# Hybrid decoder step: state space parameters made early, two accumulators for the third gate's branches, half of that gate in seven products

## The chip, the cores and the metric

The kernel runs on 1 core of one Trainium2 chip. The metric is the time of one execution in microseconds (us) of the device, as the median of several runs. A trace of one execution, which a hardware profiler took, shows every instruction of the five engines: TensorE (PE), VectorE (DVE), ScalarE (ACT), GpSimd (POOL) and SyncE (SP, which here only issues transfers).

## What is computed

One layer of a decoder for 1056 tokens (1024 of a prompt, 32 of eight samples), width 1024. The state of eight samples comes in and goes out. Cut to the parts that matter here:

```python
h = layer_norm(x) * (1 + sc1) + sh1             # sc1, sh1, ... = silu(c) @ w_ada + b_ada
proj = h @ w_in                                 # columns for four token mixers
# (A) state space layer: 16 groups of 16 channels, 64 complex states each
dt = exp(log_dt); ab = exp(dt * a_re) * (cos(dt * a_im) + 1j * sin(dt * a_im))
bb = (ab - 1) / a * b                           # parameters: no token in them
state[t] = ab * state[t-1] + bb @ u[t]
y_s = real(c @ state) + d * u
y_s = gelu(y_s);  y_a = y_s * sigmoid(y_s @ w_glu)
# (B) short gated convolution -> y_b   (C) gated delta rule -> y_c   (D) stick-breaking attention -> y_d
br = einsum('blnw,nwd->blnd', stack([y_a, y_b, y_c, y_d]), w_branch)
gates = sigmoid(h @ w_gate)                     # 4 x 1024 columns
x = layer_norm(ALPHA * x + (1 + g1) * (sum(gates * br) @ w_o))
h2 = layer_norm(x) * (1 + sc2) + sh2
x = layer_norm(ALPHA * x + (1 + g2) * (swiglu(h2 @ w_ffn_up) @ w_ffn_down))
```

## The kernel before

Features lie on the partitions, tokens in the columns, in NTB = 3 blocks of TB = 352. Each factor of a large product is held as an fp16 pair hi and lo; `mm3` issues three fp16 products for one (hi with hi, hi with lo, lo with hi). `split` makes the pair: ACT writes hi, and DVE or POOL writes lo as the difference (L108, L114, L116, L118). A 128-column weight tile takes the way wraw (fp32, loaded by SP) to whl (fp16 pair).

The tiles are issued by a scheduler at build time. It orders each engine's instructions by priorities and modelled times; `with self.sup` marks work that goes ahead of all else, `with self.lo` products that fill.

The order of the program is: `make_h`; attention (D), and inside it the short convolution (B), `ssm_u` (which stores the state space layer's input u) and the first half of the gate of B (n = 1); the delta rule (C) with the other half; then the gate of D (n = 3), the gate of C (n = 2, here called the third gate), the state space layer `ssm` (A), the sums for the seven products, the gate of A (n = 0), the output projection `mixer_out` and `ffn`.

A gate is made in one of two ways. In `gates`, an m (128 of the 1024 columns) is a direct product: for each block 24 matmuls of 352 columns into a tile of the pool gps, six matmuls of `branch` (y with w_branch) into another tile of gps, tanh on ACT (gth, L1490), the product with the branch on DVE (gth, L1494) and an addition into mix on POOL. In `gates7`, two m are made as a pair by a two-by-two scheme with seven products instead of eight (`seven`); each of the seven takes sums of weight blocks, which `pair_weights` makes (four sums on DVE, L1635 to L1643; seven lo parts on POOL, L1631; hi parts on ACT), and sums of blocks of h, which `sums7` makes on DVE once for all pairs (L1711 to L1720, with splits at L116 into the tile tf). There are six calls of `sums7`. Three of the seven products take h itself and need no sum of h. With G7 = 4 the third gate is direct for all eight m, and only the gate of A goes in pairs.

`ssm` makes its parameters first: many small operations of 8 columns (tiles sp_*), powers of the rotation cs and sn on POOL (seven rounds of a complex product, 42 operations, L1220), the tables car, cai and ab on DVE, four groups of four transposes of ab into bq, and 64 small products into k0, which goes to DRAM as kd and is read back shifted as eight tt, to which DVE adds D (L1358). Then come products of u with bq (tile sps), the scan (gg, hr and hi on DVE), the output products with tt, car and cai (sps again), gelu (gs, gx), the product with w_glu, and y_A, which is split with a stride, since the token order of the scan is another than that of the gates. The direct products of the third gate are issued ahead of `ssm` in the program, and the scheduler lays them between its products.

`ada_slab` makes 128 of the columns that scale, shift and gate: 16 small products into a tile of gps, then ACT (adat, L294) and DVE (mod, L295), both of which read PSUM. `gates` calls it once per m, `gates7` several times per pair.

The lines that the argument touches are these:

```python
    B.gates(3, B.yD, False, False, ada=A3)
    B.gates(2, B.yC, False, False, range(2 * G7), ada=A2)
    B.ssm(yp)
    ...
            B.sums7(B.h, Tf, b, g7.tile([P, 8 * HB], F32, name="r7", tag="r7"), slice(q, q + 2))
    ...
    B.gates7(2, B.yC, False, range(G7, KD // 2))
    B.gates7(0, B.yA, True, range(KD // 2))
```

## Time and profile before

| | |
|---|---|
| median of 3 runs | 1919.74 us (1913.41 to 1923.58) |
| profiled execution | 1927.88 us |
| its span, first to last instruction | 1925.8 us |
| mean granted clock of TensorE | 0.961 |
| busy: PE, DVE, ACT, POOL | 1734.6, 1297.0, 970.8, 953.9 us |
| moved by transfers | 130.60 MB, mean 68 GB/s |

All positions below are in us from the start of the span. The stages around the change lie so: attention with convolution and `ssm_u` up to about 340, delta rule and gate of D to 735, third gate and state space layer from 735 to 933, sums and gate of A to 1071, then output projection and ffn. A row of a stretch gives each engine's busy time with the number of its instructions in brackets; idle time of an engine that nothing waits for costs nothing.

### The profile page before, as it was taken

The numbers are of one execution on the slowest core, as the hardware profiler recorded it, in microseconds if no ns is written. First come the engines' busy times: TensorE is split into PE (matmuls) and PEld (weight loads), VectorE is DVE, ScalarE is ACT, GpSimd is POOL, SyncE is SP. The second block draws the span as 40 slices with busy tenths as digits, with TensorE's granted clock in tenths as the row PEclk, the third lists the DMA queues.
The fourth block names the chain that finished last, engine by engine and source line by source line (L and its number), as shares of the span: only waits on it lengthen the run. The fifth ranks groups of instructions, "written<-read, shape, count | busy, mean of one in ns | idle before, by whom it ended". The sixth has DMA issues, their size and how long they took to land.

```text
span 1925.8 us, 36541 instructions
## 1 busy us (share of the span) xinstructions
PE 1734.6 (90%) x14985; PEld 1198.5 (62%) x14985; DVE 1297.0 (67%) x2161; ACT 970.8 (50%) x1796; POOL 953.9 (50%) x952
## 2 busy tenths in 40 slices
PE   7899999999899998788689899988999998999896
PEld 3466666656566665556367555556666776767675
DVE  6763777668676765386986479677467657755748
ACT  3642454465554645235664665645445644554434
POOL 1826421222354444744541553278577667675733
PEclk9999999999999999889799999989999999999999
DMA  8222220122311112313232340001121112111112
GB/s 310 75 90 64 73 59 23 49 58 54 96 50 58 62 40 98 73 41 102 77 110 77 129 137 1 1 23 44 48 64 56 48 44 65 56 37 53 50 28 91
DMA packets 63615, 130.60 MB, mean 68 GB/s; under 512 B 16408, under 2 KB 35928, under 8 KB 63192
## 3 DMA queue, kind: packets, MB, share of 16 engines
q1 hardware_dynamic: 61912, 124.07, 20.8%
q0 software_dynamic: 1536, 4.20, 0.7%
q8 instruction: 117, 1.92, 0.4%
q14 instruction: 50, 0.41, 0.1%
HBM read 117.36 MB, written 10.88 MB: 67 GB/s over the span
## 4 chain that ended last, share of the span: by engine, by line
PE 35%; DVE 26%; POOL 12%; ACT 10%; DMA 9%; issue 7%; SPq 1%; another core or an unknown queue 0%; ACTq 0%; DVEq 0%; POOLq 0%
PE gps L87 25%; DMA wraw<-in_w_up 3%; POOL wf L1631 2%; DVE x L1903 2%; POOL whl L1631 2%; DVE ring L116 2%; PE nps L87 1%; DMA wraw<-in_w_down 1%; DVE af L1869 1%; ACT wraw L1622 1%; DVE dacc L758 1%; POOL wraw L1635 1%; PE dp L87 1%; POOL wraw L1638 1%; POOL wraw L1639 1%
## 5 line engine op out<-in xcount | busy, mean ns | idle before, releaser
L87 PEld LDWEIGHTS <-whl 128*128 128x128 f16 x6992 | 623.5, 100 | 386.1 <-issue 74.9
L87 PE MATMUL gps<-h,whl 128*128 128x352 f16 (+1 forms) x4344 | 692.9, 314 | 49.0 <-ACT ct L1683 14.8
L87 PEld LDWEIGHTS <-wf 128*128 128x128 f16 x2232 | 197.7, 99 | 71.6 <-issue 13.8
L1631 POOL TENSOR_TENSOR wf<-wraw,wf 128x512 f16<-128x512 f32 (+1 forms) x102 | 122.8, 1206 | 145.8 <-ACT wf L1630 142.9
L1631 POOL TENSOR_TENSOR whl<-wraw,whl 128x512 f16<-128x512 f32 (+1 forms) x136 | 169.2, 1250 | 47.0 <-ACT whl L1630 46.8
L114 POOL TENSOR_TENSOR whl<-wraw,whl 128x1024 f16<-128x1024 f32 (+1 forms) x66 | 149.1, 2260 | 81.2 <-ACT whl L108 79.2
L105 ACT ACTIVATE wraw<-wraw 128x1024 f32<-128x1024 f32 (+2 forms) x96 | 96.4, 1005 | 127.4 <-DMA wraw<-in_w_gate 40.1
L87 PE MATMUL gps<-tf,whl 128*128 128x352 f16 (+1 forms) x1152 | 141.1, 280 | 18.6 <-ACT ct L1683 6.9
L1622 ACT ACTIVATE wraw<-wraw 128x1024 f32<-128x1024 f32 (+1 forms) x68 | 66.5, 978 | 111.0 <-DMA wraw<-in_w_up 62.2
L1630 ACT ACTIVATE whl<-wraw 128x512 f16<-128x512 f32 (+1 forms) x136 | 79.9, 589 | 78.8 <-POOL wraw L1635 34.5
L87 PE MATMUL gps<-ring,whl 128*128 128x352 f16 (+1 forms) x864 | 103.8, 276 | 13.1 <-DVE x L1903 13.1
L87 PE MATMUL gps<-y,wbr 128*128 128x352 f16 x576 | 105.4, 319 | 8.1 <-DVE gth L1771 3.8
L1680 DVE TENSOR_TENSOR ct<-ct,gps 128x352 f32<-128x352 f32 (+1 forms) x84 | 35.4, 424 | 106.5 <-PE gps L87 90.5
L1523 POOL TENSOR_TENSOR mix<-mix,gth 128x352 f32<-128x352 f32 x48 | 54.0, 1125 | 98.0 <-DVE gth L1494 87.1
L87 PE MATMUL gps<-mix,wo 128*128 128x352 f16 x576 | 88.8, 315 | 5.7 <-DVE gth L1771 3.4
L116 DVE TENSOR_TENSOR ring<-af,ring 128x352 f16<-128x352 f32 (+2 forms) x134 | 82.0, 645 | 7.8 <-ACT ring L108 7.7
L108 ACT ACTIVATE whl<-wraw 128x1024 f16<-128x1024 f32 (+1 forms) x82 | 84.8, 1035 | 4.4 <-DMA wraw<-in_w_ada 3.5
L87 PE MATMUL gps<-h,wf 128*128 128x352 f16 (+1 forms) x624 | 79.4, 283 | 6.6 <-DVE gth L1494 5.5
L87 PEld LDWEIGHTS <-wbr 128*128 128x128 f16 x576 | 56.5, 99 | 39.2 <-issue 10.2
L87 PEld LDWEIGHTS <-wo 128*128 128x128 f16 x576 | 56.7, 99 | 38.6 <-issue 5.9
L108 ACT ACTIVATE ring<-af 128x352 f16<-128x352 f32 (+2 forms) x134 | 52.2, 427 | 46.4 <-DVE af L1869 30.4
L87 PE MATMUL gps<-tf,wf 128*128 128x352 f16 (+1 forms) x528 | 66.6, 283 | 3.8 <-ACT cu L1683 3.6
(625 smaller groups left out, 3381.4 us busy)
## 6 DMA issues: line engine op xcount, KB each, us to landing
wraw<-in_w_up SPq DMA_DIRECT2D x44, 512.0 KB, 3.5
wraw<-in_w_gate SPq DMA_DIRECT2D x32, 512.0 KB, 3.9
wraw<-in_w_ada SPq DMA_DIRECT2D x32, 512.0 KB, 3.5
wraw<-in_w_in SPq DMA_DIRECT2D x20, 512.0 KB, 4.0
wraw<-in_w_down SPq DMA_DIRECT2D x24, 384.0 KB, 3.1
x<-in_xT SPq DMA_DIRECT2D x12, 704.0 KB, 7.7
araw<-in_w_ada SPq DMA_DIRECT2D x16, 512.0 KB, 10.9
wraw<-in_w_branch SPq DMA_DIRECT2D x8, 512.0 KB, 3.5
```

The source lines that it names most:

```text
L87: self.nc.tensor.matmul(out, lhsT=lhsT, rhs=rhs, start=start, stop=stop, skip_group_check=resume)
L105: nc.scalar.activation(src, src, AF.Copy, scale=scale)
L108: nc.scalar.activation(hi, src, AF.Copy, scale=scale)
L114: nc.gpsimd.tensor_tensor(lo, src, hi, op=ALU.subtract)
L116: nc.vector.tensor_tensor(lo, src, hi, op=ALU.subtract)
L758: nc.vector.scalar_tensor_tensor(acc[:, :L], ext[:, k:k + L], wts[:, i, k:k + 1], acc[:, :L], op0=ALU.mult, op1=ALU.add)
L1523: nc.gpsimd.tensor_tensor(o, o, g, op=ALU.add)
L1622: nc.scalar.activation(raw, raw, AF.Copy, scale=SW)
L1630: nc.scalar.activation(hi, src, AF.Copy)
L1631: nc.gpsimd.tensor_tensor(lo, src, hi, op=ALU.subtract)
L1680: add = lambda o, p: nc.vector.tensor_tensor(o, o, p, op=ALU.add)
L1903: nc.vector.scalar_tensor_tensor(x[:, h, z], part(h, z), gate[:, m, 0:1], x[:, h, z], op0=ALU.mult, op1=ALU.add)
```

## The change

1. G7 goes from 4 to 2. The third gate's m 0 to 3 stay direct, ahead of `ssm`; m 4 to 7 become two pairs in `gates7`, behind the six `sums7`. `ada_slab` is called four times less in `gates` and that many times more in `gates7`.
2. `gpb`, a PSUM pool of two banks, holds the branch products from the third gate until `ssm` is issued; in exchange sps has three banks instead of five.
3. The parameters of `ssm` move to `ssm_prep`, called in the attention ahead of `ssm_u`. Their results go to DRAM (spt, kd, with D already added in kd) and are loaded again at the head of `ssm`, before its products.
4. `ada_slab` copies all 18 columns out of PSUM with one ACT operation of top priority, and DVE adds from SBUF.
5. The tail of y_A is written in token order into a tile yt by two DVE operations, and one contiguous split follows for each half.

```diff
-G7 = 4
+G7 = 2
...
-            t = self.cp.tile([P, 9], F32, name="adat", tag="adat", bufs=2)
-            nc.scalar.activation(t, ps[:, 9:18], AF.Identity, scale=c, bias=self.b_ada[:, m:m + 1])
-            nc.vector.scalar_tensor_tensor(self.mod[:, m], ps[:, 0:9], c, t, op0=ALU.mult, op1=ALU.add)
+            t = self.cp.tile([P, 18], F32, name="adat", tag="adat", bufs=2)
+            with self.sup:
+                nc.scalar.activation(t, ps[:, 0:18], AF.Copy, scale=c)
+            nc.vector.scalar_tensor_tensor(self.mod[:, m], t[:, 0:9], self.b_ada[:, m:m + 1], t[:, 9:18],
+                                           op0=ALU.add, op1=ALU.add)
...
+    def ssm_prep(self):
...
+        def put(name, src, o=0):
+            d = self.spd(name)
+            nc.sync.dma_start(d[:, o:o + src.shape[1]], src)
...
+                V.tensor_tensor(k0[q, :, 112:128], k0[q, :, 112:128], dg[q], op=ALU.add)
+                nc.sync.dma_start(kd.rearrange("h (a e) c -> e h a c", e=2)[e][:, ha], k0[q])
...
-            p_ = pp.tile([P, 512], F32, name="sps", tag="sps", bufs=5)
+            p_ = pp.tile([P, 512], F32, name="sps", tag="sps", bufs=3)
...
+        with self.sup:
+            nc.sync.dma_start(U, self.su)
+            nc.sync.dma_start(bq.rearrange("p a j c -> p (a j c)"), self.spd("bq"))
+            nc.sync.dma_start(cs.rearrange("p a c -> p (a c)"), self.spd("cs"))
+            nc.sync.dma_start(sn.rearrange("p a c -> p (a c)"), self.spd("sn"))
+            nc.sync.dma_start(m8, self.spd("m8"))
+            for j in range(8):
+                nc.sync.dma_start(tt[16 * j:16 * j + 16], self.kd[:, :, 112 - 16 * j:240 - 16 * j])
+            nc.sync.dma_start(car.rearrange("p a k o -> p (a k o)"), self.spd("car"))
+            nc.sync.dma_start(cai.rearrange("p a k o -> p (a k o)"), self.spd("cai"))
+            nc.sync.dma_start(p4.rearrange("p i a -> p (i a)"), self.spd("p4"))
...
-            V.scalar_tensor_tensor(th, th, 1.0, ys[i], op0=ALU.add, op1=ALU.mult)
-            tv = th.rearrange("p (j c) -> p j c", j=8)
-            pv = lambda j: yA[:, j, i, 0:NP].rearrange("p (c j) -> p j c", j=8)
-            sv = lambda j: yA[:, j, i, NP:TOK].rearrange("p (b t) -> p t b", t=DS)
-            self.split(pv(0), pv(1), tv[:, :, 0:P], SA / 4)
-            self.split(sv(0), sv(1), tv[:, 0:4, P:W], SA / 4)
+            yt = pq.tile([P, TOK], F32, name="yt", tag="gx2")
+            jv = lambda z: z.rearrange("p (j c) -> p j c", j=8)
+            V.scalar_tensor_tensor(yt[:, 0:NP].rearrange("p (c j) -> p j c", j=8), jv(th)[:, :, 0:P], 1.0,
+                                   jv(ys[i])[:, :, 0:P], op0=ALU.add, op1=ALU.mult)
+            V.scalar_tensor_tensor(yt[:, NP:TOK].rearrange("p (b t) -> p t b", t=DS), jv(th)[:, 0:4, P:W], 1.0,
+                                   jv(ys[i])[:, 0:4, P:W], op0=ALU.add, op1=ALU.mult)
+            self.split(yA[:, 0, i], yA[:, 1, i], yt, SA / 4)
...
-        pb = self.gtile2()[:, :TB]
+        pb = (self.gpb or self.gp2).tile([P, 512], F32, name="gpb" if self.gpb else "gps", tag="gpb" if self.gpb else "gps")[:, :TB]
...
+        with B.br:
+            B.ssm_prep()
         B.ssm_u()
+        B.free(B.ssm_par)
...
+    B.gpb = B.pool("gpb", bufs=2, space=PSUM)
     B.gates(2, B.yC, False, False, range(2 * G7), ada=A2)
     B.ssm(yp)
+    B.free(B.gpb)
+    B.gpb = None
```

The first place in the built order is DVE around gelu and the tail of y_A. Lines move by the change: gelu is L1447 to L1450 before and L1509 to L1512 after, the sums are L1711 to L1720 before and L1774 to L1783 after. Before:

```order
L1447 TENSOR_SCALAR gs<-gs 128x1088
L1448 TENSOR_TENSOR gs<-gs,gx 128x1088
L1711 TENSOR_TENSOR r_11464<-h 128x352 x2
L1712 TENSOR_TENSOR r_11464<-r_11464 128x352
L1494 SCALAR_TENSOR_TENSOR gth<-gth,gps 128x352
L1715 TENSOR_TENSOR r_11464<-r_11464 128x352
L1450 SCALAR_TENSOR_TENSOR gx<-gs,gx 128x1088
L1716 TENSOR_TENSOR r_11464<-r_11464 128x352
```

After, from the second half of gelu on:

```order
L1512 SCALAR_TENSOR_TENSOR gx<-gs,gx 128x1088
L118 SCALAR_TENSOR_TENSOR yh<-gx,yh 128x1088
L1529 SCALAR_TENSOR_TENSOR yt<-gs,gx 128x4x8
L1527 SCALAR_TENSOR_TENSOR yt<-gs,gx 128x8x128
L118 SCALAR_TENSOR_TENSOR y<-yt,y 128x1056
L1527 SCALAR_TENSOR_TENSOR yt<-gs,gx 128x8x128
L1529 SCALAR_TENSOR_TENSOR yt<-gs,gx 128x4x8
L118 SCALAR_TENSOR_TENSOR y<-yt,y 128x1056
L1774 TENSOR_TENSOR r_10940<-h 128x352 x2
L1775 TENSOR_TENSOR r_10940<-r_10940 128x352
```

The first sums of h stood between the operations of gelu; now all six stand behind the last split of y_A. In SBUF the second yt and tf overlap by 288 bytes of a partition.

The second place is SP's queue at the head of `ssm`; out_delta_p is the last store of the delta rule. Before:

```order
L1126 DMA out_delta_p<-u 128x128
L142 DMA wraw<-in_w_gate 128x1024
L1207 DMA U<-ssu 128x2320
L1231 DMA par<-in_ssm_par 128x552
L142 DMA wraw<-in_w_ada 128x1024
L142 DMA wraw<-in_w_gate 128x1024
```

After:

```order
L142 DMA wraw<-in_w_gate 128x1024
L1413 DMA U<-ssu 128x2320
L1414 DMA bq<-spt 128x2048
L1415 DMA cs<-spt 128x1032
L1416 DMA sn<-spt 128x1032
L1417 DMA m_10565<-spt 128x8
L1419 DMA tt<-kd 16x16x128 x8
L1420 DMA car<-spt 128x1152
L1421 DMA cai<-spt 128x1152
L1422 DMA p_10569<-spt 128x16
L1467 DMA h_10680<-in_st_ssm 128x128
```

The load of the raw parameters (par) is gone from here to the attention, and the loads of their results stand in its place in one row; kd and tt were issued later before, when kd was there.

## Rows read from the trace of the kernel before

**Rows 1.** The page: busy us (share of the span) and instructions of each engine.

```profile
PE 1734.6 (90%) x14985; PEld 1198.5 (62%) x14985; DVE 1297.0 (67%) x2161; ACT 970.8 (50%) x1796; POOL 953.9 (50%) x952
```

**Rows 2.** Stretches: us, busy us (instructions) by engine, granted clock, DMA share, GB/s.

```profile
96.00:240.00 144.00, 134.67 (x1105) 92.78 (x1104) 80.70 (x144) 57.40 (x109) 66.17 (x142) 0.96 0.25 76
240.00:340.00 100.00, 99.28 (x844) 65.61 (x842) 74.36 (x86) 46.90 (x83) 19.86 (x37) 1.00 0.16 39
735.00:803.00 68.00, 54.15 (x376) 36.15 (x374) 39.63 (x116) 28.65 (x47) 53.03 (x59) 0.87 0.22 77
909.00:979.00 70.00, 45.42 (x327) 27.93 (x324) 64.91 (x72) 42.66 (x66) 39.18 (x27) 0.78 0.29 98
979.00:1071.00 92.00, 86.62 (x838) 65.36 (x837) 62.31 (x117) 51.28 (x105) 20.50 (x15) 0.96 0.24 76
```

**Rows 3.** The chain of waits from 735 to 1075: start, us, what.

```profile
743.26 5.42 DMA par<-in_ssm_par
...
799.53 4.51 PE sps L87 x48
...
826.40 1.23 DVE gg L1220
...
856.51 3.07 DVE hi L1220
...
909.49 1.95 DVE gs L1463
...
922.63 4.83 ACT y L108
927.48 5.33 DVE y L118 x2
...
1014.09 49.42 PE gps L87 x467
```

**Rows 4.** Timeline of PE, three pieces: start, us, instructions [idle before <-releaser].

```profile
734.60 3.74 PE L87 MATMUL gps<-h,whl 128*128 128x352 f16 x24
...
793.35 2.82 PE L100 MATMUL sps<-ident,ab 128*128 128x128 f32 x12 [6.88 <-DVE ab L1220]
...
798.44 1.06 PE L87 MATMUL gps<-y,wbr 128*128 128x352 f16 x6
```

**Rows 5.** The list of transfers, that of U: issues, KB each, us to landing.

```profile
U<-ssu SPq DMA_DIRECT2D x1, 1160.0 KB, 5.1
```

**Rows 6.** Timeline of DVE from 930 to 985, columns as in rows 4.

```profile
932.70 1.91 DVE L1711 TENSOR_TENSOR r<-h 128x352 f32<-128x352 f16 x2
...
974.04 2.17 DVE L118 SCALAR_TENSOR_TENSOR whl<-wraw,whl 128x1024 f16<-128x1024 f32 x1
...
978.38 1.21 DVE L118 SCALAR_TENSOR_TENSOR whl<-wraw,whl 128x1024 f16<-128x1024 f32 x1
...
981.85 0.52 DVE L116 TENSOR_TENSOR tf<-r,tf 128x352 f16<-128x352 f32 x1
```

**Rows 7.** Groups of DVE's instructions from 735 to 1071: busy us, mean ns.

```profile
L118 DVE SCALAR_TENSOR_TENSOR whl<-wraw,whl 128x1024 f16<-128x1024 f32 x16 | 23.3, 1456 | 0.0
...
L1711 DVE TENSOR_TENSOR r<-h 128x352 f32<-128x352 f16 x12 | 14.1, 1214 | 0.0
...
L1720 DVE TENSOR_TENSOR r<-r 128x352 f32<-128x352 f32 x6 | 3.1, 517 | 0.1
```

**Rows 8.** PE's matmuls by form over the span, one group.

```profile
L87 PE MATMUL gps<-h,whl 128*128 128x176 f16 x480 | 44.7, 239 | 0.0
```

**Rows 9.** What PE waits for from 96 to 240: us, times, longest.

```profile
PE z L87 <- ACT th L469: 4.3, 2, 3.4
PE wtp L100 <- DVE th L476: 2.7, 2, 2.5
```

**Rows 10.** What PE waits for from 735 to 1071, columns as in rows 9.

```profile
PE gps L87 <- DVE gth L1494: 13.3, 5, 5.5
PE gps L87 <- ACT gth L1490: 9.9, 3, 5.2
```

191 lines of the change are left out of this document (114 added, 77 removed).

## The prediction

> **What bounds the kernel now.** I read the shares of busy time first: TensorE (PE) is busy 1734.6 us of the 1925.8 us span [rows 1]. A change that leaves TensorE's work nearly as it is can then only win idle time, so the next view is the table of stretches [rows 2]. The reader is to see in it where TensorE rests: it is busy 134.67 of 144 us and 99.28 of 100 us in the attention stretches, but 54.15 of 68 us (735 to 803, while the state space parameters are made) and 45.42 of 70 us at a granted clock of 0.78 (909 to 979, while the sums for the seven products are made). From 979 to 1071 it is busy 86.62 of 92 us. Third, the chain of waits [rows 3]: the state space layer is one long chain. Its parameters land at 748.7 and are worked on until the small products end at 804, the input products follow, the scan begins with gg at 826.40 and its last hi ends at 859.6, the output products, gelu and glu run to 909, and the strided splits of y_A end at 932.8. From 1014 to the end of the stretch the chain is TensorE's own. So there are two bounds in a row: the state space chain, which TensorE fills with the direct products of the third gate (n = 2, started at 734.60 [rows 4]), and behind it VectorE's sums, which let the seven products of the last gate begin in earnest.
>
> **The change, part by part.** All sums are made on the profiled execution (1927.88 us, of which 1925.8 are span); the median of the runs shown is 1919.74, which is 8.1 us less, and at the end I take these off.
>
> *Parameters moved into the attention.* Their work leaves 743 to 803. What is left of it is a reload: U, bq, cs, sn, m8, eight tt, car, cai, p4 and h0, about 5.45 MB by their shapes. Issued near 743 as U is now, and at the pace at which parameters landed (282 KB by its shape, in 5.42 us [rows 3]) this alone would take 105 us; at the best pace of wide transfers (U's 1160 KB in 5.1 us [rows 5]) 24 us. These are its bounds; U is the same kind of transfer, so I take 24, add 6 for the eight tt in small rows, and get 773. The input products need only the first two loads, start near 753 and take as long as now (804 to 826, with fillers between them), so they end near 777, and gg starts there instead of at 826.40: 49 us earlier. gg also stands behind copies that wait for p4 and h0, the last two loads, so the reload decides this number. From gg to the end of hi stays 33.2 us (826.40 to 859.6), and the further chain to the end of glu 49.1 us; three of the six sums stood in that piece on VectorE and now stand behind it, for which I take 6 off. The end of glu comes near 777 + 33 + 43 = 853.
>
> *The tail of y_A.* Its splits are strided: 4.83 us on ACT for the second half, 5.33 on VectorE [rows 3], and the same again for the first half. They become two short operations and one contiguous split per half; the nearest rows for the pieces are VectorE's 1.21 and 2.17 us for a contiguous 128x1024 split [rows 6]. I count 7 us instead of 24. y_A is complete near 860 instead of 932.8: 73 us earlier.
>
> *Six sums behind one another.* Here the gain meets VectorE. Before, three sums were done while gelu ran, and the other three with eight weight splits and eight pair sums took from 932.70 to 982.4 [rows 6]. Now yt lies on the bytes of tf's start, and the order shows all six behind the last yt. The six lines of a sum, from 14.1 us for L1711 to 3.1 for L1720 [rows 7], make 47.0; seven ada splits of 1.456 us are 10.2; eleven pair sums at some 1.1 us are 12. That makes 69 us, so the sixth sum ends near 860 + 69 = 929: 53 us earlier than 982, not 73. If every operation ran at its short duration (the two pieces of L1711 at 1.91, the eight others near 0.52, the splits at 1.21 [rows 6], the pair sums at 0.52 x 512 / 352) it would be 53 us; that is the lower bound. I take 69, since the row of the same work is 49.7 us for three sums.
>
> *Half of the third gate moved behind.* Four of its eight m leave the stretch in which they filled TensorE's waits. A direct m costs three blocks of 3.74 us [rows 4] and their branch products, 1.06 us each. As pairs in seven products they cost 84 products of 352 columns at 0.156 us (3.74 / 24) and 84 of 176 columns at 0.093 (44.7 / 480 [rows 8]), 20.9 us per pair against 22.4 direct. So the saving by arithmetic is 1.5 us per pair, 3 us in all. The two pairs with their 12 groups of branch products come to 54.5 us that now stand behind glu. TensorE in the stretch ahead loses its cover, but that is no loss in itself, since the chain has its own pace there; it simply idles more.
>
> *The end of the gates.* At 982 some 89 us were left to 1071. With the sixth sum at 929, the same 89 us and the 54.5 us follow. From them goes what TensorE can do in the wait: it ran 45.42 of 70 us at clock 0.78 in the like wait of before [rows 2], and the wait is now 69 us from 860 where it was 46 from 936, so some 10 us more get done (none if the sums of the last block release the most, 20 if the products of h alone fill it). 44.5 us at the pace of 92 / 86.62 are 47. The end comes at 929 + 89 + 47 = 1065, between 1054 and 1076, where it was 1071: 6 us earlier.
>
> *The price in the attention.* The parameters' TensorE work goes there: 16 transposes, twelve of which took 2.82 us [rows 4], and 64 small products, 48 of which took 4.51 [rows 3], so 3.8 + 6.0 = 9.8 us, and up to 40 us of VectorE (39.63 from 735 to 803 [rows 2]), as well as the 42 GpSimd operations of cs and sn. TensorE idles 9.3 us in 96 to 240 and 0.7 us in 240 to 340 [rows 2], so the bounds are 0 (all of it falls into this idle time) and 10, plus what late scans add; the waits there are for th on ACT and VectorE [rows 9], which shows that the idle time belongs to a chain that VectorE could lengthen. I take 7, nearer to 10 because almost no time is free. Its 26 stores and the reload pass SP's queue, whose other loads at that place are ahead by several tiles.
>
> *The accumulators and the ada slabs.* Branch products get two PSUM banks of their own, sps has three banks instead of five, and an ada slab gives its bank back after a copy on ACT. TensorE's waits for gth were 13.3 and 9.9 us from 735 to 1071 [rows 10]. Most lie where the chain, not TensorE, sets the end, so I count nothing; the bound is a gain of some 5 us. Three sps banks could also cost the output products a wait of up to 3 us.
>
> *Sum:* -6 + 7 = +1 us, so 1929 for the profiled execution, and against the median 1919.74 + 1.0, taken as **1921 us**.
>
> **A rule on the contention.** In the trace the same 128x1024 split on VectorE takes 2.17 us while GpSimd works on the weight forms and 1.21 us a little later [rows 6]. The Trainium skill, "SBUF — State Buffer", section "Who interferes with whom", says that a VectorE instruction with two SBUF inputs and a GpSimd instruction that reads SBUF take the shared port pair by turns, each for its whole length. By this rule the 69 us fall toward 53 wherever GpSimd rests; the trace agrees with the two durations, and the rule is part of the first rival's case.
>
> **The rivals.** (a) *The sums keep the gain.* If VectorE runs the six sums near its short durations, the sixth ends at 913 and the end of the gates comes 16 us earlier; with 5 us more if the attention hides its part, that is 1921 - 16 - 5 = 1900. For it: VectorE is otherwise empty from 860 on, and the splits' mean of 1.456 us [rows 7] lies nearer to 1.21 than to 2.17. Against it: POOL must write the lo forms of the pairs in just that stretch (39.18 of 70 us busy there [rows 2]). (b) *Attention pays*, the slower side: VectorE's 40 us and the extra PSUM tiles lengthen the chain of th scans behind which the attention's products wait (4.3 and 2.7 us now [rows 9]). If TensorE's idle time in 96 to 240 doubles, it costs 9.3 on top of the 10, so 19 instead of 7: 1921 + 12 = 1933, up to 1940 if the weight splits on POOL queue behind the 42 operations too. From 15 us in the attention on, it decides the sign. Against it: VectorE is busy 80.70 of 144 us there, so there is room. (c) *The reload doesn't do what it should*: p4 and h0 land late, since each small tt row costs, and gg starts near 797; every later time moves by 20 us, less what TensorE does in the meantime, some 10: 1931 to 1941.
>
> **How the numbers follow.** My forecast has a chance of 0.46 with its own range from 1909 to 1934, by the bounds of the gate end (-11, +11) and of the attention (-7, +3); (a) 0.29 at 1890 to 1908; (b) 0.15; (c) 0.10. Half a per cent, 9.6 us, is about what a measurement of this kernel tells from no change: 1910 to 1929. Of the forecast 0.07 lies below, 0.27 within and 0.12 above; (a) lies below; (b) gives 0.13 above and 0.02 within; (c) 0.06 above and 0.04 within. That makes faster 0.36, same 0.33, slower 0.31. The range leaves out the outer tenth on either side: 1896 to 1943.
>
> **What would show it.** In the changed kernel's profile gg should start near 777 and y_A be complete near 860 after the attention's shift; if gg starts after 795, the reload is the wrong step. VectorE should be full for about 69 us behind the last yt, with TensorE idling at a lower clock beside it; if the sixth sum ends within 55 us, (a) is right. From the first direct product of the third gate to the end of the last gate should take about 330 us (734.60 to 1071, 336, before), and the time up to that first product should have grown by some 7 us; if it grew by over 15, (b) is right. A granted clock that stays high behind y_A would make the 45 us of fill wrong.

## The result: 26 us slower, and the loss lies ahead of the state space layer

The changed kernel takes **1945.32 us** (median of 4 runs, 1942.95 to 1947.57), the kernel before 1918.84 in the runs beside it: a ratio of **1.0146**, interval 1.0130 to 1.0162. The forecast was 1921, with a range that ended at 1943. The profiled execution took 1942.95 us, 1941.2 of them span.

The page of the changed kernel, busy us, share of the span and instructions by engine, answers to [rows 1]:

```profile
PE 1736.3 (89%) x15033; PEld 1202.6 (62%) x15033; DVE 1303.4 (67%) x2191; ACT 964.9 (50%) x1812; POOL 950.4 (49%) x959
```

TensorE is busy for 1.7 us more than before, in a span that is 15.4 us longer. The work is the same; what grew is the time in which TensorE rests. The stretches of the changed kernel say where (columns as in [rows 2]; attention twice, then gg's approach to the last yt, the six sums, and the gates behind them):

```profile
96.00:240.00 144.00, 127.49 (x1023) 87.24 (x1021) 97.86 (x226) 56.45 (x109) 89.37 (x180) 0.95 0.26 85
240.00:340.00 100.00, 95.62 (x825) 64.32 (x826) 76.20 (x101) 48.49 (x88) 22.18 (x38) 1.00 0.21 58
756.00:884.00 128.00, 98.52 (x698) 65.80 (x692) 55.23 (x80) 51.96 (x115) 38.77 (x30) 0.89 0.37 103
884.00:948.00 64.00, 36.40 (x272) 21.93 (x273) 62.25 (x90) 34.47 (x65) 34.01 (x26) 0.68 0.28 91
948.00:1083.00 135.00, 131.43 (x1274) 99.38 (x1271) 84.58 (x151) 73.36 (x151) 52.32 (x40) 1.00 0.26 83
```

In 96 to 240 TensorE was busy 134.67 us before [rows 2] and is now at 127.49, with 82 instructions fewer, while VectorE rose from 80.70 to 97.86 and POOL from 66.17 to 89.37. The chain of waits of the changed kernel (start, us, what; pieces from 776 to the end of the gates) shows the state space layer much as forecast, only later:

```profile
776.85 5.22 DMA U<-ssu
782.08 10.39 DMA tt<-kd
792.49 6.22 DMA h<-in_st_ssm
...
882.88 1.26 DVE y L118
...
1042.36 34.17 PE gps L87 x315
```

Set side by side, in us from the start of the span (the third column is an experiment, in which the making of the parameters is left out and only its stores and the reload stay):

| place | before | changed | changed, parameters not made |
|---|---|---|---|
| first addition into mix (gate of B) | 282.6 | 320.9 | 281.5 |
| last product of the delta rule | 721.6 | 756.1 | 723.9 |
| gg | 826.4 | 801.0 | 768 |
| y_A complete | 932.8 | 884.1 | 851 |
| sixth sum | 982 | 948 | 920 |
| first product of the output projection | 1073.2 | 1083.0 | 1054.6 |

The changed kernel is 38 us late when the gate of B adds its first block and still 34.5 us late when the delta rule ends. The state space layer and the sums win back 24.7 us of it by the output projection, where it is 9.8 us late. The rows of the first and third place, of the changed kernel and then of the one without the parameters (duration in ns: least, median, most; first and last start in us):

```profile
L1555 DVE SCALAR_TENSOR_TENSOR mix<-gth,gps x24: 492/514/522, 320.9 to 534.0; 128x352 f32<-128x352 f32 x24
...
L87 PE MATMUL dp<-qk_t,S x120: 186/193/259, 613.7 to 756.1; 64*64 64x64 f16 x120
```

```profile
L1414 DVE SCALAR_TENSOR_TENSOR mix<-gth,gps x24: 494/514/522, 281.5 to 506.8; 128x352 f32<-128x352 f32 x24
...
L87 PE MATMUL dp<-qk_t,S x120: 192/193/260, 583.9 to 723.9; 64*64 64x64 f16 x120
```

The profiled execution of before was one of its longer ones (1927.88 against a median of 1918.84), so differences of traces come out some 10 us smaller than the ratio says. Below, prices are read from ratios to the kernel before on the same chip; 0.1% is 1.9 us.

### The profile page after: what moved, and what is told of

Same layout as the page of the kernel before. It is cut to its first block, busy times and chain, and to the rows that moved or that the text cites. A ratio compares the mean times of both kernels' runs of the same rounds, so it can differ in the third digit from the quotient of the medians.

```text
span 1941.2 us, 36735 instructions
## 1 busy us (share of the span) xinstructions
PE 1736.3 (89%) x15033; PEld 1202.6 (62%) x15033; DVE 1303.4 (67%) x2191; ACT 964.9 (50%) x1812; POOL 950.4 (49%) x959
## 4 chain that ended last, share of the span: by engine, by line
PE 36%; DVE 27%; POOL 11%; DMA 10%; ACT 9%; issue 6%; SPq 1%; ACTq 0%; DVEq 0%; POOLq 0%
PE gps L87 27%; DMA wraw<-in_w_up 3%; POOL wf L1694 2%; POOL whl L1694 2%; DVE x L1966 2%; DVE ring L116 2%; DMA wraw<-in_w_gate 1%; PE nps L87 1%; PE dp L87 1%; DVE af L1932 1%; DMA wraw<-in_w_down 1%; DVE dacc L761 1%; PE x L87 1%; PE sps L87 1%; PE pada L87 1%
## 5 line engine op out<-in xcount | busy, mean ns | idle before, releaser
L87 PEld LDWEIGHTS <-whl 128*128 128x128 f16 x6896 | 611.7, 99 | 374.4 <-issue 74.7
L87 PE MATMUL gps<-h,whl 128*128 128x352 f16 (+1 forms) x4104 | 644.4, 310 | 33.0 <-ACT ct L1746 15.3
L87 PEld LDWEIGHTS <-wf 128*128 128x128 f16 x2376 | 208.5, 99 | 74.2 <-issue 8.2
L1694 POOL TENSOR_TENSOR whl<-wraw,whl 128x512 f16<-128x512 f32 (+1 forms) x144 | 179.1, 1251 | 63.3 <-ACT whl L1693 56.3
L87 PE MATMUL gps<-tf,whl 128*128 128x352 f16 (+1 forms) x1296 | 160.9, 282 | 24.5 <-ACT ct L1746 7.7
L114 POOL TENSOR_TENSOR whl<-wraw,whl 128x1024 f16<-128x1024 f32 (+1 forms) x58 | 134.7, 2322 | 92.1 <-ACT whl L108 80.5
L105 ACT ACTIVATE wraw<-wraw 128x1024 f32<-128x1024 f32 (+2 forms) x88 | 87.9, 1000 | 96.7 <-DMA wraw<-in_w_gate 29.6
L87 PE MATMUL gps<-y,wbr 128*128 128x352 f16 x504 | 93.9, 322 | 14.8 <-DVE ct L1743 7.1
L87 PE MATMUL gps<-h,wf 128*128 128x176 f16 (+1 forms) x720 | 90.1, 280 | 8.0 <-ACT wf L1693 6.6
L1746 ACT ACTIVATE ct<-gps 128x352 f32<-128x352 f32 (+1 forms) x156 | 57.0, 379 | 40.6 <-PE gps L87 40.6
```

Source lines behind the costliest of these rows:

```text
L87: self.nc.tensor.matmul(out, lhsT=lhsT, rhs=rhs, start=start, stop=stop, skip_group_check=resume)
L105: nc.scalar.activation(src, src, AF.Copy, scale=scale)
L114: nc.gpsimd.tensor_tensor(lo, src, hi, op=ALU.subtract)
L1694: nc.gpsimd.tensor_tensor(lo, src, hi, op=ALU.subtract)
L1746: nc.scalar.activation({0: c11, 2: c12, 3: c22}[f], ps, AF.Copy)
```

## Experiments on the price in the attention

**Everything of it left out.** In the changed kernel the raw parameters are loaded and one memset makes what is stored; transposes, small products, VectorE's and POOL's operations of the parameters go.

```diff
-        x, y = t8("x"), t8("y")
-        V.tensor_scalar(x, dt, -1.0 / 128, None, op0=ALU.mult)
...
-                bq = stage()[:, 0:512]
-                nc.scalar.activation(bq, ps, AF.Copy)
-                put("bq", bq, (a0 + a) * 256)
+        W = work()
+        G.memset(W, 0.125)
+        for n, c in self.SPD:
...
+                put(n, W[:, 0:d], o)
```

> The changed kernel, with the making of the parameters left out: the early step only loads the raw parameters, sets one tile to a constant and makes the same stores; the later reload stays. Left out are thus some 40 us of VectorE work, the 42 GpSimd operations of cs and sn, 16 transposes and 64 small products. Theory 1 (the price lies in the attention: the parameters' operations stand in VectorE's queue ahead of what TensorE waits for there): the first addition to mix comes back by some 25 to 38 us, to 283 to 296 us from the start of the span where it was 282.6 before and 320.9 with the change, and the whole is 24 to 34 us faster than the changed kernel, 1911 to 1921 us. Theory 2 (the price lies behind, in the seven products moved behind the state space layer or in the new ada slabs): 0 to 10 us faster, 1935 to 1945 us.

Measured: 1905.56 us, 0.9921 (0.9904 to 0.9937), against 1.0146 for the changed kernel with the work. By these two ratios the making of the parameters in the attention costs 2.25%, **some 43 us** (40 by the medians), where the forecast had 7. Theory 1 holds, with more than its 24 to 34 us. The loss stands in stages that use none of the values left out, so it is not one of the values. By the traces 32 of the 43 us are there when the delta rule ends. From the start to that point, of the changed kernel and then of the one without the parameters (columns as in [rows 2]):

```profile
0.00:756.10 756.10, 691.47 (x6637) 449.37 (x6639) 526.03 (x936) 367.81 (x640) 310.50 (x421) 0.96 0.25 80
```

```profile
0.00:723.90 723.90, 674.10 (x6530) 438.67 (x6530) 488.76 (x813) 358.31 (x622) 281.87 (x377) 0.96 0.26 82
```

TensorE is busy 17.4 us longer and idle 14.8 us longer (64.6 against 49.8). Its own part is in the groups of its matmuls from 75 to 330 (columns as in [rows 8]), 10.0 us, as forecast (9.8):

```profile
L87 PE MATMUL gps<-spw,bd 64*16 64x128 f32 x64 | 7.7, 270 | 0.0
...
L100 PE MATMUL gps<-ident,spw 128*128 128x128 f32 x16 | 2.3, 279 | 0.0
```

So 22 of the 32 us are not the work itself: 15 of waiting, and 7 in which the other products took longer or other fillers came in; which of these two was not separated. Where the waiting stands: the stretch from 75 to 150 and the worst 25 us of it, of the changed kernel and then of the one without the parameters (columns as in [rows 2]):

```profile
75.00:150.00 75.00, 54.69 (x365) 36.03 (x365) 64.67 (x174) 37.33 (x77) 52.80 (x82) 0.89 0.29 96
125.00:150.00 25.00, 14.58 (x115) 11.06 (x115) 24.84 (x41) 4.46 (x10) 22.13 (x31) 0.85 0.35 119
```

```profile
75.00:150.00 75.00, 67.91 (x512) 47.90 (x512) 46.60 (x99) 39.71 (x85) 36.58 (x70) 0.95 0.28 86
125.00:150.00 25.00, 25.00 (x227) 20.06 (x225) 11.19 (x26) 6.27 (x17) 6.74 (x28) 1.00 0.10 34
```

From 125 to 150 VectorE has no free time (24.84 of 25) and POOL hardly any (22.13), and TensorE falls from 25.00 to 14.58. What stands on VectorE there (start, us, instructions):

```profile
125.22 5.14 DVE L1224 TENSOR_TENSOR spw<-par,piv 128x576 f32<-128x576 f32 x4
...
137.64 1.41 DVE L1224 TENSOR_TENSOR spw<-par,prv 128x576 f32<-128x576 f32 x2
...
140.52 1.83 DVE L1348 SCALAR_TENSOR_TENSOR spw<-spw 128x576 f32<-128x576 f32 x2
```

And what TensorE waits for from 75 to 160 (us, times, longest), of the changed kernel and then of the one without the parameters:

```profile
PE gps L87 <- DVE qS L409: 7.2, 1, 7.2
PE po L87 <- DVE vt L110: 6.5, 1, 6.5
PE po L87 <- DVE wt L116: 2.7, 1, 2.7
```

```profile
PE gps L87 <- DVE qS L409: 4.0, 2, 3.1
PE wtp L100 <- DVE th L479: 2.1, 1, 2.1
PE gps L87 <- POOL h L114: 1.4, 1, 1.4
```

All waits of this stretch come to 22.3 us against 7.5, which is as much as the 14.8 us of idle time. The wait for qS is there without the parameters too, and grew by 3 us; the one for vt is new. TensorE goes on at 135.64, when a cast of vt that takes 0.42 us by itself is done: in VectorE's queue it stood at 135.17, behind the four 576-column products (5.14 us) and what had piled up behind them. This is the mechanism of rival (b), with other small pieces than its th scans.

**One part left out at a time**, each time in the changed kernel: the wide VectorE operations (the tables car, cai and ab), TensorE's part (transposes and small products), POOL's 42 operations of cs and sn.

```diff
-            tt_(V, car, cw(cc[:, 0]), pw(prv), ALU.mult)
...
-            tt_(V, ab[:, 0], pw8(prv), cw8(bd[:, 0]), ALU.mult)
...
+            G.memset(W, 0.125)
```

> The changed kernel without VectorE's wide parameter operations: the 26 operations of 512 and 576 columns that make car, cai and ab are left out and two GpSimd memsets of their tile stand for them; the operations of 8 to 128 columns, cs and sn, the transposes and the small products stay. If VectorE's wide operations are the price, most of the 40 us comes back: 1908 to 1920 us. If the price is shared by the many small ones, by GpSimd and by TensorE, a third or less: 1930 to 1942 us.

```diff
-                for a in range(4):
-                    for j, c in ((0, car), (1, cai)):
-                        self.mm(ps[32 * e:32 * e + 16, a], bd[r, j, a0 + a], c[r, a, 0:8].rearrange("p k o -> p (k o)"),
...
-                        self.tr(pv[:, q, j], ab[:, j, a + q].rearrange("p j h -> p (j h)"))
```

> The changed kernel with TensorE's part of the early parameters left out: the 16 transposes and the 64 small products, near 10 us of TensorE, and their six tiles in the three gps banks; a memset and copies of the same shapes stand for them, and everything on VectorE and GpSimd stays. If TensorE's time is the remaining price, it takes its 10 us and what the held banks cost besides, 10 to 16 us of the 40: 1929 to 1935 us. If VectorE's queue is nearly all of it, 1940 to 1946 us.

```diff
-        for l in range(7):
...
-            cmul(G, cs[:, :, n + 1:2 * n + 1], sn[:, :, n + 1:2 * n + 1], cs[:, :, 1:n + 1], sn[:, :, 1:n + 1],
+        G.memset(W, 0.125)
```

> The changed kernel with the 42 GpSimd operations of cs and sn left out (one memset stands for them). They stand between the masks of the attention and the lo parts of weights on GpSimd from 115 to 150 us. If GpSimd's queue, or VectorE operations held up beside GpSimd, carry a part of the price: 6 to 14 us faster than the changed kernel, 1931 to 1939 us. If not: 1942 to 1947 us.

Measured: 1936.19 us without the wide operations (1.0096, 1.0073 to 1.0119), 1932.06 without TensorE's part (1.0069, 1.0052 to 1.0085), 1938.26 without cs and sn (1.0102, 1.0085 to 1.0119). Against 1.0146 that is 10, 15 and 8 us, each within the range put for a part of the price and each uncertain by 4 to 5 us. No single engine carries the price; added up, the three make 33 of the 43 us, but the next run shows that they may not be added.

**The small operations left out.** This takes out the hundred-odd operations of 8 columns on VectorE, and ACT's exp and sin; memsets stand in for seven of their results.

```diff
-        x, y = t8("x"), t8("y")
...
-        V.tensor_tensor(fi, fi, den, op=ALU.mult)
+        m8, c1, s1 = t8("m8"), t8("c1"), t8("s1")
```

> The changed kernel with the small parameter operations left out: some 100 VectorE operations of 8 to 128 columns and the exponentials and sines on ACT, from the raw parameters to bd, prv and piv; seven GpSimd memsets stand for them, and the wide operations, cs and sn, the transposes and the small products stay. By theory 1 (all of VectorE's queue counts, and each small operation there takes its turn ahead of the attention's) the unexplained 11 us are theirs: 1929 to 1937 us. If the parts are not additive (the chain of parameters only matters as a whole): 1920 us or less. If they carry nothing: 1941 to 1946 us.

Measured: 1954.0 us, 1.0186 (1.0154 to 1.0218), so 8 us *slower* than with them, which none of the three cases allowed. Two rows of TensorE's waits from 75 to 350 grew:

```profile
PE gps L87 <- DVE qS L409: 11.2, 1, 11.2
PE wtp L100 <- DVE th L479: 8.2, 5, 3.5
```

It waits 11.2 us for qS, 7.2 in the changed kernel, and 8.2 for th, 2.1 there, while the 6.5 for vt are gone. Without the small operations the wide ones become ready earlier and stand ahead of qS; one of 576 columns took 6.89 us at 86.84 there. So the parts are not terms of a sum: to leave one out moves the others, and here it is the th scans of rival (b) that TensorE waits for. What the small operations cost by themselves stays open.

**The block moved.** If the price came from the place (the narrow 75 to 150), a later one should save most of it. A copy from a late tile into the target of the parameters' load holds the whole block back until the gate inputs of the delta rule (ba) are there; the text put on record names another late tile, but the edit takes ba.

```diff
         par = pq.tile([P, 552], F32, name="par")
+        G.tensor_copy(par[:, 0:1], self.ba[:, 0, 8:9])
         nc.sync.dma_start(par, I["ssm_par"])
```

> The changed kernel with the load of the raw parameters held back until the last value tile of the attention is there, by a small GpSimd write into its tile, so that the same parameter operations run near 165 to 250 us, where VectorE was 11.56 and 12.96 of 25 us busy, and not from 79 to 150 us, where it is 64.67 of 75 us busy with the change. Theory 1 in its narrow form (VectorE's queue between 79 and 150 us is what costs): half or more of the 40 us comes back, 1915 to 1928 us. Rival (TensorE's own 10 us of parameter products and the stores on SP's queue cost, wherever they stand): 1935 to 1950 us.

Measured: 1954.4 us, 1.0188 (1.0166 to 1.0210), 8 us slower than at the old place and slower than both cases. The delta rule ends at 766.4, 10 us later than in the changed kernel. The stretches of this kernel:

```profile
75.00:150.00 75.00, 68.49 (x516) 48.00 (x515) 45.53 (x99) 37.64 (x79) 35.66 (x74) 0.97 0.28 90
...
150.00:175.00 25.00, 19.57 (x137) 13.22 (x136) 20.22 (x94) 6.32 (x14) 19.39 (x61) 0.94 0.19 61
...
200.00:225.00 25.00, 19.98 (x156) 12.08 (x156) 19.15 (x20) 8.94 (x16) 22.17 (x24) 0.86 0.28 93
...
250.00:275.00 25.00, 21.55 (x136) 14.06 (x135) 21.89 (x34) 10.20 (x18) 4.89 (x9) 0.73 0.18 51
```

75 to 150 is as fast as without the parameters (68.49 against 67.91 us of TensorE), and the loss has moved with the block: 5.4, 5.0 and 3.5 us of idle TensorE in three of the stretches that follow, and a lower clock in the last. My theory that the place made the price fell here: TensorE is nearly full in all of the attention [rows 2], and the block cost at both places tried.

## Experiments on the half gate and the early parameters

**Early parameters only**, on the kernel before, and their counterpart, the changed kernel with the parameters made inside `ssm` as before.

```diff
+        self.ssm_par = self.pool("ssm_par", side="right")
...
+    def ssm_prep(self):
...
+        with B.br:
+            B.ssm_prep()
```

> The kernel before with the early parameters alone: third gate all direct, five banks for the output products, old ada slabs, old tail of y_A. Theory 1: the attention costs what it costs in the changed kernel (first addition to mix near 318 to 322 us), and the gain behind is small, since the direct products of the third gate, not the chain, then fill the stretch until near the end of glu: 1925 to 1940 us. Theory 2 (the cost lies in the half gate): the early parameters alone gain what they take from the chain, 1895 to 1912 us.

> The changed kernel, with the parameters made at the head of the state space layer as before; half of the third gate in seven products, the two accumulators, the ada slabs and the new tail of y_A stay. Theory 1: the attention is as before (first addition to mix near 283 us), but the chain from the third gate to y_A is some 50 us longer, with only four direct m to fill it: y_A near 915 us, the six sums 64 us after it, 135 us of the gates behind, so the first product with w_o near 1105 to 1115 us and the whole 1950 to 1960 us, slower than the changed kernel. Theory 2 (moving half of the gate is harmless and the parameters alone cost): 1910 to 1920 us.

Measured: 1918.81 us for the early parameters alone, 0.9997 (0.9984 to 1.0009), no change; 1971.29 for the changed kernel without them, 1.0264 (1.0247 to 1.0281). Neither case of the first text holds (1925 to 1940, 1895 to 1912); the second run is slower than its theory 1 (1950 to 1960). What the attention pays and what the shorter chain gives back cancel on the kernel before: with the early parameters the delta rule ends at 764.5, 43 us later, gg starts at 799.1, 27 earlier, and the output projection at 1066.0, 7 earlier than in the long profiled execution of before. In the changed kernel, where fewer direct products cover the chain, the early parameters are worth 1.2%, 22 us, in spite of their price.

**The half gate undone**, by one number, with the parameters made (first), without their making (second), and with the block held back (third).

```diff
-G7 = 2
+G7 = 4
```

> The changed kernel with all eight m of the third gate direct (G7 = 4), all else as changed. Theory 1 (the attention's price is the loss, and the gain behind it depends on the cover): the attention stays at its price (first addition to mix near 321 us) and the direct m fill the chain's waits as in the early parameters alone, so within 8 us of those, 1910 to 1927 us. Theory 2 (half of the gate in seven products costs by itself, whatever stands in the attention, as the 1971.29 us without early parameters suggest): the same time. If the half gate is a gain once the chain is short, it is slower than the changed kernel, over 1950 us.

> The making of the parameters left out as in the first run, and all eight m of the third gate direct. Against that run's 1905.56 us it tells what the half gate is worth when the attention pays nothing. Theory 1 (the half gate costs since TensorE lacks cover in front and has 54 us more behind): 10 to 20 us faster than that run, 1886 to 1896 us, as the 19 us between the changed kernel and the one with eight direct m say. Rival (the half gate is a gain as soon as the chain starts early enough): slower than that run, 1908 to 1920 us.

> The changed kernel with both: all eight m of the third gate direct, and the raw parameters' load held back as in the run before. By theory 1 the two gains add where they lie in different stretches: 15 to 25 us under the run with eight direct m, 1893 to 1910 us, faster than the kernel before. If the attention's price stays, 1910 to 1927 us.

Measured: 1926.25 us (1.0032, 1.0020 to 1.0045), 1893.6 (0.9865, 0.9849 to 0.9882) and 1927.2 (1.0038, 1.0018 to 1.0058). The first two came as theory 1 said; the third fell just above the case in which the attention's price stays. So the half gate costs 1.14%, 22 us, in the changed kernel; 0.56%, 11 us, where the attention is free of the parameters; and 1.5%, 29 us, with the block held back. The forecast had it save 3 by arithmetic. Read the other way, the same runs price the making of the parameters at 1.67%, 32 us (1.0032 against 0.9865), where the gate is direct; there the delta rule ends 40 us later with it (760.1 against 719.7). So the price is 32 to 43 us, by what stands behind it. How it goes is seen best in the pair without the attention's price. From gg to y_A and from there to the output projection, with the gate direct (763 to 880, then to 1040):

```profile
763.00:880.00 117.00, 107.03 (x775) 72.74 (x774) 61.65 (x74) 50.33 (x103) 55.17 (x34) 0.95 0.29 88
880.00:1040.00 160.00, 127.50 (x1135) 89.89 (x1133) 127.48 (x202) 83.83 (x169) 63.73 (x44) 0.85 0.24 80
```

and with half of it in pairs (768 to 850, then to 1054):

```profile
768.00:850.00 82.00, 63.18 (x413) 42.60 (x411) 47.33 (x60) 32.01 (x74) 26.62 (x18) 0.89 0.25 72
850.00:1054.00 204.00, 170.18 (x1544) 122.19 (x1545) 149.77 (x240) 111.12 (x218) 92.47 (x67) 0.89 0.26 83
```

With four direct m more, the chain from gg to y_A takes some 117 us and TensorE works in 107 of them; without them it takes some 82 and TensorE idles for 19. So the direct products do hold the chain, by 35 us, but 44 us of TensorE's work comes out of that stretch, and it is paid for behind y_A: 204 us instead of 160. The half gate trades 35 us ahead for 44 behind; gg began 5 us later besides (4 of them are there when the delta rule ends, 723.9 against 719.7), and the output projection 14.5 later.

## Experiments on the accumulators, the ada slabs and the tail of y_A

**The new tail on the kernel before**, first as the change has it (yt of 1056 columns, which reaches 288 bytes into tf), then in two halves of 512 and 544 columns, so that yt and tf do not overlap, and the same halves in the changed kernel.

```diff
-            self.split(pv(0), pv(1), tv[:, :, 0:P], SA / 4)
-            self.split(sv(0), sv(1), tv[:, 0:4, P:W], SA / 4)
+            yt = pq.tile([P, TOK], F32, name="yt", tag="gx2")
...
+            self.split(yA[:, 0, i], yA[:, 1, i], yt, SA / 4)
```

> The kernel before with the new tail of y_A alone (token order into yt, one contiguous split per half). My estimate: the tail shrinks from 24 to some 12 us, but yt lies on tf's start and moves sums behind it; between 8 us faster and 4 us slower, 1911 to 1923 us. If the overlap pushes all six sums behind the tail, the sums take 64 us from there and it is 10 to 20 us slower.

```diff
+            for c0 in (0, 64):
+                n = 512 + (NS if c0 else 0)
+                yt = pq.tile([P, 512 + NS], F32, name="yt", tag="gx2")
...
+                self.split(yA[:, 0, i, 8 * c0:8 * c0 + n], yA[:, 1, i, 8 * c0:8 * c0 + n], yt[:, 0:n], SA / 4)
```

> The kernel before with the new tail of y_A alone, and yt in two halves, so that the sums stay free to run between gelu's operations. The tail alone ended y_A 20 to 29 us earlier but had its six sums behind it and gained nothing. If the sums were what took the gain: 8 to 15 us faster than before, 1904 to 1912 us. If TensorE's own work from there sets the end: 1914 to 1920 us.

> The changed kernel with yt in two halves of 512 and 544 columns, so that it ends below the place of tf: the order then has the first sums between gelu's operations again. My prediction had the overlap as the reason that all six sums (64 us in the changed kernel's trace, from 884 to 948) stand behind y_A. If VectorE's sums behind y_A set the end, two of them taken out of this stretch give back 10 to 20 us: 1925 to 1935 us. If TensorE's 135 us of gates behind set it by themselves, 0 to 5 us: 1940 to 1945 us.

Measured: 1921.45 us for the tail as it is (1.0007, 0.9996 to 1.0017), **1905.83 in halves (0.9939, 0.9912 to 0.9967)**, and 1941.35 for halves in the changed kernel (1.0106, 1.0086 to 1.0126). In halves the tail is worth 12 us on the kernel before, whole it is worth nothing. The traces show why; splits of the sums into tf, whole and then in halves:

```profile
L116 DVE TENSOR_TENSOR tf<-r,tf x27: 508/518/2205, 909.8 to 1266.2; 128x352 f16<-128x352 f32 x24, 128x704 f16<-128x704 f32 x3
```

```profile
L116 DVE TENSOR_TENSOR tf<-r,tf x27: 508/518/1478, 882.2 to 1260.1; 128x352 f16<-128x352 f32 x24, 128x704 f16<-128x704 f32 x3
```

Whole, y_A is complete at 905, but the first split into tf comes only at 909.8, the sixth sum ends at 978.5 and the output projection begins at 1067.1. In halves the splits run from 882.2 on, between gelu's operations: y_A is complete only at 919, and yet the sixth sum ends at 955.3 and the output projection begins at 1055.1. A whole yt without the overlap was not run, so the smaller pieces may have a part in it. In the changed kernel the halves give 8 us by the ratios, whose intervals leave 1 to 15, but their traces do not show it: the sixth sum ends 10 us earlier (937.6 against 948), y_A is complete 13 later (897 against 884.1), and the output projection begins at 1083.8 against 1083.0. By its range this is the second case, in which TensorE's work behind the sums sets the end. The forecast saw the overlap (all six sums behind the last yt) but put no price of its own on it. Among the versions that compute the whole layer, the halves alone on the kernel before gain most.

**The smaller edits together**, on the kernel before (accumulators, ada slabs, the whole tail), then two of them alone on top of the halves.

```diff
-            p_ = pp.tile([P, 512], F32, name="sps", tag="sps", bufs=5)
+            p_ = pp.tile([P, 512], F32, name="sps", tag="sps", bufs=3)
...
+    B.gpb = B.pool("gpb", bufs=2, space=PSUM)
```

> The kernel before with the three small edits alone: two accumulators with three banks for the output products, ada slabs that are copied first, the new tail of y_A. The tail alone measured no change. If the accumulators and ada slabs cost the 7 us that lie between the early parameters alone and all of the change with eight direct m: 1924 to 1930 us. If these arise only together with the early parameters (the sums pushed behind y_A by the overlap): 1914 to 1921 us.

> The kernel before with the tail of y_A in two halves, and the two accumulators with three banks for the output products. If the three banks stretch the products with u and the output products (30 and 26 us against 24 and 16), and this is the price: 1916 to 1924 us, and the output products again take some 26 us. If not: within 4 us of 1905.83.

> The kernel before with the tail of y_A in two halves and the new ada slabs. If the ada slabs gain what TensorE waits for mod (7.9 us in that trace): 1898 to 1904 us. If they carry a part of the 17 us: 1910 to 1920 us. If neither: within 3 us of 1905.83.

Measured: 1936.13 us for all three (1.0090, 1.0064 to 1.0117), slower than both cases; on the halves, 1918.75 with the accumulators (1.0006, 0.9994 to 1.0018) and 1914.21 with the ada slabs (0.9984, 0.9974 to 0.9995). Against 0.9939 the accumulators cost 0.67%, 13 us, and the slabs 0.45%, 9 us. The output products, with five sps banks (halves alone) and with three (accumulators added):

```profile
L87 PE MATMUL sps<-hi,cai x32: 274/277/381, 852.7 to 867.6; 64*128 64x137 f32 x32
```

```profile
L87 PE MATMUL sps<-hi,cai x32: 277/277/592, 864.1 to 891.8; 64*128 64x137 f32 x32
```

The same 32 products begin 11 us later and stretch over 27.7 instead of 14.9 us. TensorE does not stand still there: the order lays 13 us of the third gate's products between groups of 18 output products, where with five banks they follow one another. Eighteen are three tiles of six products, and there are three banks; that the banks made this order is argued, not measured. One wait for a bank shows ahead of the scan, where the products with u wait until ACT (si) has read one; from 720 to 850, accumulators added:

```profile
PE sps L87 <- ACT si L1383: 3.7, 1, 3.7
```

With halves alone no such row is there. Most of the loss stands ahead of the output products: gg begins at 836.7 against 819.5, with 3 of these 17 us there at the end of the delta rule; y_A is complete 22 us later, and the output projection begins 14 later (1069.4 against 1055.1). For the slabs the stretch from 905 to 980, of the halves and then with the slabs:

```profile
905.00:980.00 75.00, 50.34 (x439) 34.52 (x439) 70.11 (x99) 44.78 (x85) 45.32 (x30) 0.84 0.32 103
```

```profile
905.00:980.00 75.00, 51.02 (x382) 33.87 (x381) 69.77 (x90) 42.74 (x80) 43.94 (x31) 0.78 0.33 106
```

TensorE is as busy beside VectorE's sums with the slabs as without, with 57 instructions fewer at a lower clock. Of the 9 us between the two spans 6 are there when gg begins (825.7 against 819.5), and as many when the output projection begins (1060.8 against 1055.1). What makes gg late was not found, nor which of the slab's two new operations.

**Early parameters and halves together**, on the kernel before.

> The early parameters and the new tail with yt in halves, on the kernel before: all eight m direct, no accumulators of their own, old ada slabs. With the early parameters alone, the six sums were done before y_A and y_A ended at 936 us of 1917.5, so a shorter tail lies on the path: 8 to 14 us under the early parameters alone, 1905 to 1911 us. If TensorE's direct products fill the tail anyway: 1915 to 1921 us.

Measured: 1913.8 us, 0.9976 (0.9953 to 0.9998), its runs from 1904.4 to 1921.4. That lies between the two cases. It is no better than the halves alone, which fits the early parameters' zero.

## Why the forecast was wrong, step by step

| step of the forecast | forecast | without the parameters' making | changed kernel |
|---|---|---|---|
| gg, from the end of the delta rule | 55 (722 to 777) | 44 | 45 |
| gg to y_A | 83 | 83 | 83 |
| y_A to the sixth sum | 69 | 69 | 64 |
| sixth sum to the output projection | 136 to the end of the gates | 134 | 135 |
| price in the attention | 7 | 0 by construction | 32 at the end of the delta rule and 28 at the output projection against the column ahead, some 43 by the ratios |

**The step that failed is the price in the attention**: 7 us, with bounds of 0 and 10, against some 43 by leaving it out. Three things were wrong in it. The upper bound was TensorE's own work, 9.8 us (10.0 measured), and "what late scans add" stood in the sentence without a number, so that the bound held nothing for waits. The room was read from a mean, VectorE's 80.70 of 144 us [rows 2] and its 39.63 us of work as though they would spread, where the work stood as a block: 24.84 of 25 us from 125 on. And POOL's operations were only given 7 us, in the upper end of a rival. The waits for th [rows 9], 4.3 and 2.7 us, had shown that TensorE depends on short VectorE pieces there. In the changed kernel th itself is waited for less in that stretch (0.9 and 0.8 us), and vt and wt are waited for instead, with qS ahead of it; the whole price is six times the 7 us. A part of the miss was hidden by luck: from the end of the delta rule to the output projection the forecast has 343 us and the changed kernel takes 327, 10 of the difference in gg and 5 in the sums. By the forecast's own sign the place is plain: the first direct product of the third gate comes near 764 instead of 734.6, 30 us later, where over 15 was to mean rival (b).

**Rival (b), attention pays**, had the mechanism and the sign, at a chance of 0.15 and 1933 to 1940. It doubled TensorE's idle time of 9.3 us in 96 to 240; measured, that went to 16.5 there, 0.7 went to 4.4 in 240 to 340, and 18.8 to 21.9 ahead of 96, where the wait for qS stands (the forecast did not read it). With TensorE's own 10 these make 24 us, where it had 19; what its price left out besides is the 7 us by which the other products' time grew. It put its upper end at 1940, and the time is 1945. Rival (c), the late reload, did not happen: gg came 45 us behind the delta rule, earlier than the forecast's 55. Its sign (gg after 795) is met by 801.0 only through the attention's delay of 34.5 us. The reload itself, from U to h, took 22 us on the chain of waits above, where the forecast had 30. Rival (a), short sums, hardly: 69 and 64 us, nearer to 69 than to 53. The groups of VectorE's instructions from 884 to 950 (columns as in [rows 7]) show which part of a sum was shorter in the changed kernel:

```profile
L118 DVE SCALAR_TENSOR_TENSOR whl<-wraw,whl 128x1024 f16<-128x1024 f32 x8 | 11.6, 1453 | 0.0
L1774 DVE TENSOR_TENSOR r<-h 128x352 f32<-128x352 f16 x12 | 11.2, 975 | 0.1
```

The splits kept their mean (1453 ns against 1456 [rows 7]), the first line of a sum fell from 1214 to 975 ns.

**The gate end, -6.** Without the attention's price the output projection began at 1054.6, 18.6 us earlier than in the profiled execution of before; the forecast had 6, so this step was right in kind and some 12 us too cautious: 9 in gg (768 against 777), 2 behind the sums, and 2 because the forecast ended the gates of before at 1071, where the output projection began at 1073.2. The fill behind y_A was put too high: TensorE did 36.40 us at a clock of 0.68 in the changed kernel's wait, 4 more than the 32.15 in the wait of before (932.8 to 982.4), where the forecast had 10 more; it then worked 131.43 of 135 us, a better pace than the forecast's 86.62 of 92, so 135 against 136 is again partly luck.

The half gate was counted as a gain of 3 us by arithmetic, and it costs 11 to 29. The work moved behind was sized well: 47 us put there, and 44 measured from y_A to the output projection between the two kernels without the parameters. What failed is the sentence that the chain has its own pace ahead whatever TensorE does: with the direct gate the same early gg (763) reaches y_A only near 880, so taking half of the gate out gives back 35 us there. That is still less than the 44, and with the direct gate the output projection begins earlier (1040 against 1054.6).

**Counted at nothing, accumulators and slabs.** The forecast allowed a gain of 5 us, and a loss of 3 for the sps banks. On the halves they cost 13 and 9. The gth waits of [rows 10] were no hint of a gain, since they lay where the chain set the end, as the forecast itself said; the sps banks lie on the chain. The 3 us for the banks were put at the output products, and most of the measured loss stands ahead of gg. What they cost inside the changed kernel was not measured alone.

**The overlap of yt and tf** was read from the order and priced only as a place of six sums; whole against in halves, it stands for 13 us on the kernel before (1.0007 against 0.9939) and for 8 by the ratios in the changed one, which the traces there do not show.

**Two slips in the working** have no part in the miss: the parameters' stores are 16 in the changed kernel's list of transfers, not 26, and by the bounds named beside it the forecast's own range would be 1903 to 1935, not 1909 to 1934.

**Open.** The share of the small operations; why the slabs cost; whether the banks or the order of the fillers made the accumulators' price; and 6 to 9 us behind the output projection's start, where the same products take 858 us in the changed kernel, 853 before and 849 without the parameters.

## What to carry to other kernels

A block of vector work moved under a stage in which the matrix engine is nearly full is not hidden by the mean idle time of the vector engine: price it by the short pieces that the matrix engine waits for, and by the longest stretch for which the block would fill the vector engine, and do not put the upper bound at the matrix engine's own part. Fewer buffers on the chain that sets the end (here sps, five to three) cost 13 us together with the two banks they paid for; a gain from the waits elsewhere, which such banks were to remove, did not show. And look where a new tile lies: the tail of y_A gained 12 us only in the form that shares no bytes with the next stage's tile.

## What the runs showed of the hardware that was not expected

In the changed kernel an operation on eight columns lasted 6.41 us on VectorE; the timeline of VectorE and then that of POOL from 84 to 92 (start, us, instructions):

```profile
84.49 6.41 DVE L1245 TENSOR_SCALAR sp_y<-sp_y 128x8 f32<-128x8 f32 x1
```

```profile
84.59 4.20 POOL L114 TENSOR_TENSOR wv<-wraw,wv 128x1024 f16<-128x1024 f32 x2
88.74 2.12 POOL L114 TENSOR_TENSOR whl<-wraw,whl 128x1024 f16<-128x1024 f32 x1
```

It ended at 90.90, as POOL's third 1024-column operation did at 90.86, and qS stood behind it in VectorE's queue: this is the 7.2 us wait above. The same operation on the same shape took 0.17 at 92.18. The early parameters did not bring this hold in. In the kernel before, the same three operations of POOL run from 84.09 to 90.38, and another operation of VectorE is held:

```profile
85.33 5.61 DVE L116 TENSOR_TENSOR kh<-kr,kh 128x512 f16<-128x512 f32 x1 [0.90 <-ACT kh L108]
```

TensorE waits 3.8 us for qS there. With the parameters a small operation gets into that place earlier, with fewer pieces of qS done ahead of it. With the block moved, where the small operations stand at 151 beside POOL's short copies, the held one (here L1246) is short:

```profile
L1246 DVE TENSOR_SCALAR sp_y<-sp_y x3: 171/195/223, 151.1 to 152.0; 128x8 f32<-128x8 f32 x3
```

The Trainium skill, "SBUF — State Buffer", section "Who interferes with whom", says that a VectorE tensor_scalar can enter a mode that uses the port pair it shares with GpSimd, and that whichever of the two engines issues first then holds the pair for its whole instruction while the other blocks fully. The trace agrees in the end times, and adds that three such instructions in a row held one small operation. By the records VectorE's operation began 0.10 us ahead of POOL's first and was yet the one held, which the trace does not explain.
